# Attention on one Trainium2 core: four logit products issued together with banks of two PSUM pools, and weight transpositions written one block ahead of the value products

## The chip, the core and the metric

The kernel runs on one core of one Trainium2 chip. TensorE (PE) multiplies matrices and writes its results to PSUM, which has eight banks of 512 float32 columns on each of 128 partitions. VectorE (DVE) and ScalarE (ACT) read those banks and compute in SBUF, GpSimd (POOL) adds a little, and DMA queues bring weights from HBM. The metric is the device time of one execution in microseconds; the time of a kernel is the median of its runs.

## What is computed

Two layers of a backbone over 256 context tokens and 256 latent tokens of width 1024. Each layer is a half-step SwiGLU, three token mixers side by side (attention, a gated linear attention and an mLSTM) that are merged by sigmoid gates, and a second half-step SwiGLU. The change touches attention alone. It has 8 query heads of width 64 on 2 key and value heads. Context tokens look at the context; latent tokens look at a window of 128 latent tokens to either side and at the whole context. Each head has a sink logit that takes part in the softmax only. Cut to the latent part:

```python
s_loc = jnp.einsum('bnqhgd,bnkhd->bnhgqk', qb, kb).astype(F32) * scale
s_ctx = jnp.einsum('bnqhgd,bchd->bnhgqc', qb, k_ctx).astype(F32) * scale
s_loc = jnp.where(valid[None, :, None, None], s_loc, -jnp.inf)
p = softmax_with_sink(jnp.concatenate([s_loc, s_ctx], axis=-1), sink_b)
o = (jnp.einsum('bnhgqk,bnkhd->bnqhgd', p_loc, vb)
     + jnp.einsum('bnhgqc,bchd->bnqhgd', p_ctx, v_ctx))
```

## The kernel before

Channels lie on partitions and the 512 tokens (256 of context, then 256 latent) along the free axis. Large products take weights split into a high and a low float32r part and need three matmuls each (`mm3`, lines 258 to 260): high weight by high input, high weight by low input, low weight by high input. A dense product of 128 output channels is 8 x 3 = 24 such matmuls into one bank of the `acc` pool. PSUM's eight banks are shared out in two pools of four: `pacc`, which `acc()` draws from, and `pmx`, which `mx()` draws from and which serves everything small.

The instructions are written in program order; a scheduler then lays out a fixed queue for each engine. It takes the earliest written instruction whose inputs and buffers it expects to be there, so later work that is free goes ahead of earlier work that waits. Between engines semaphores keep the order of data and buffers. On the chip each queue runs in its order.

`attention` (line 1100 on) works in units. A unit is a pair index `a` (0 or 1) and a block of 128 query tokens `qt`: in layer 0, 2 x 4 units, called units 1 to 8 here; in layer 1, where only the latent tokens are wanted, 2 x 2 units, called 1 to 4. Within a group of one `a` the context blocks come first. A unit has four heads: `b` (0, 1) times `kv` (0, 1), where `kv` sets whether rows 0 to 63 or 64 to 127 of the queries `aq[2 * a + b]` and of the keys `kh` are contracted.

- `weights(a, qt)` forms the logits of each head with one matmul (line 1123) of 64 rows into one bank: 256 columns for a context block, 512 for a latent one. It is a float32 product that the trace records as two passes. For a latent block a mask is added (line 1126); then come the maximum (line 1127), its negative against the sink (line 1128), the exponential with its sum on ScalarE (line 1130) into a tile `p` of the 17 tiles of tag `t`, and, after the four heads, the normalisation (lines 1132 to 1138). A logit bank is free once its exponential is done.
- `values(a, qc, nk, pp)` goes over the blocks of 128 keys, two for a context unit and four for a latent one. For each block it transposes the four heads' weights into one bank (line 1147), copies that to SBUF (line 1150 on VectorE for odd blocks, line 1152 on ScalarE for even ones), and multiplies by the values, 64 output channels for each `kv` (line 1154), into the bank `po`, which is copied out at the end (line 1157).
- `fill()` forms one of the eight products of the branch gate "sa" (a dense product into an `acc` bank and a tanh, line 1263); in layer 1 a unit calls for two.

The loop at the end of `attention` writes the weights of a unit, then the fill, then the values of the unit before. The gates, and behind attention the branch "sm", are what the scheduler draws forward where attention waits.

Of the kernel before, what the change touches and what calls it, by code (L numbers as in the profile page):

```python
# [77 lines left out]
def hybrid_backbone_kernel(ctx: ExitStack, tc: tile.TileContext, xT, cc, small, tables, lmask, crow, modw, modt,  # L78
# [20 lines left out]
    def nm(p):  # L99
        cnt[0] += 1  # L100
        return f"{p}{cnt[0]}"
# [4 lines left out]
    def W(dt=F32):  # L106
        return tp.tile([128, T], dt, tag="t", name=nm("t"))

    def O(dt=F32):
        return ox.tile([128, T], dt, tag="x", name=nm("x"))  # L110
# [7 lines left out]
    def mx():  # L118
        return pmx.tile([128, T], F32, tag="mx", name=nm("mx"))

    tt, act, mm = V.tensor_tensor, A.activation, PE.matmul
# [35 lines left out]
    def C(n, i=None, w=128):  # L157
        o, ww = CT[n]
        return ct[:, o:o + ww] if i is None else ct[:, o + i * w:o + (i + 1) * w]
# [13 lines left out]
    def P(l, n, i=0, w=1):  # L173
        o, _ = SM[n]
        return sm[l][:, o + i:o + i + w]
# [896 lines left out]
    def rope(x):  # L1072
        ls = slice(L, T)
        ps = mx()
        mm(ps[:, ls], C("perm"), x[:, ls], True, True)
        t = W()
        tt(t[:, ls], ps[:, ls], C("sin"), ALU.mult)
        tt(x[:, ls], x[:, ls], C("cos"), ALU.mult)
        tt(x[:, ls], x[:, ls], t[:, ls], ALU.add)
# [20 lines left out]
    def attention(l, c0, aq, kh, vt, fill):  # L1100

        rope(kh)
        for i in range(4):
            rope(aq[i])
        nsink = sp.tile([128, 8], F32, tag="nsink", bufs=1, name="nsink%d" % l)
        V.tensor_scalar(nsink[:], P(l, "sink", 0, 8), -1.0, None, ALU.mult)
        sink = P(l, "sink", 0, 8).rearrange("p (v j) -> p v j", v=2)
        ao = [O() for _ in range(4)]

        def weights(a, qt):  # L1110
            lat = qt >= 2
            nk = T if lat else L
            qc = slice(qt * 128, (qt + 1) * 128)
            mx4 = sp.tile([128, 4], F32, tag="mx4", bufs=3, name=nm("mx4"))
            l4 = sp.tile([128, 4], F32, tag="l4", bufs=3, name=nm("l4"))
            e4 = sp.tile([128, 4], F32, tag="e4", bufs=3, name=nm("e4"))
            pp = [None] * 4
            for b in range(2):
                for kv in range(2):
                    h, j = 4 * kv + 2 * a + b, 2 * kv + b  # L1120
                    r = slice(64 * kv, 64 * kv + 64)
                    ps = mx()
                    mm(ps[:, 0:nk], aq[2 * a + b][r, qc], kh[r, 0:nk], True, True)  # L1123
                    if lat:
                        blk = slice(L + 128, T) if qt == 2 else slice(L, L + 128)
                        tt(ps[:, blk], ps[:, blk], C("amask", qt - 2), ALU.add)
                    V.reduce_max(mx4[:, j:j + 1], ps[:, 0:nk], axis=AX.X)
                    V.scalar_tensor_tensor(mx4[:, j:j + 1], mx4[:, j:j + 1], -1.0, nsink[:, h:h + 1], ALU.mult, ALU.min)
                    p = W()
                    act(p[:, 0:nk], ps[:, 0:nk], AF.Exp, bias=mx4[:, j:j + 1], accum_out=l4[:, j:j + 1])  # L1130
                    pp[j] = p
            tt(e4[:].rearrange("p (v j) -> p v j", v=2), sink[:, :, 2 * a:2 * a + 2],
               mx4[:].rearrange("p (v j) -> p v j", v=2), ALU.add)
            act(e4[:], e4[:], AF.Exp)
            tt(l4[:], l4[:], e4[:], ALU.add)
            V.reciprocal(l4[:], l4[:])
            for j in range(4):
                V.tensor_scalar(pp[j][:, 0:nk], pp[j][:, 0:nk], l4[:, j:j + 1], None, ALU.mult)
            return a, qc, nk, pp

        def values(a, qc, nk, pp):
            nb = nk // 128
            po = mx()
            for kb in range(nb):
                pt = mx()
                for j in range(4):
                    PE.transpose(pt[:, j * 128:(j + 1) * 128], pp[j][:, kb * 128:(kb + 1) * 128], C("ident"))  # L1147
                t = W()
                if kb % 2:
                    V.tensor_copy(t[:], pt[:])  # L1150
                else:
                    A.copy(t[:], pt[:])
                for kv in range(2):
                    mm(po[64 * kv:64 * kv + 64, 0:256], vt[:, kb * 128 + 64 * kv:kb * 128 + 64 * kv + 64],  # L1154
                       t[:, 256 * kv:256 * kv + 256], kb == 0, kb == nb - 1)
            for b in range(2):
                V.tensor_copy(ao[2 * a + b][:, qc], po[:, b * 128:(b + 1) * 128])

        last = None
        for a in range(2):  # L1160
            for qt in range(c0 // 128, 4):
                now = weights(a, qt)
                fill()
                if last:
                    values(*last)
                last = now
        fill()
        values(*last)
        return ao

# [349 lines left out]
```

## Time and profile before

| what | value |
|---|---|
| median of 3 runs | 2302.86 us (2300.45 to 2303.84) |
| the profiled execution | 2299.65 us |
| its span, first to last instruction | 2297.5 us |
| TensorE busy | 2269.5 us, 99% of the span |
| VectorE busy | 1532.1 us, 67% |
| ScalarE busy | 970.8 us, 42% |
| attention, layer 0 | about 772 to 859 us |
| attention, layer 1 | about 1988 to 2039 us |

The profile is one execution. A timeline line gives the start of a group of instructions, its length, the engine, the line of the kernel, the operation, output and inputs by the program's names, the shapes (for a matmul rows x columns of the stationary operand first) and how many follow one another without another line between. Matmuls are pipelined: one that starts 0.24 us after the last may be shown as 0.4 us long, so times of TensorE are read from start to start. "PEld" is its loading of weights.

### The profile page before, as it was taken

The page shows a single profiled execution, that of the slowest core. Times are in us where ns is not written, and L with a number is a line of the kernel's source. Part 1 is how long each engine was busy: PE and PEld are TensorE (multiplying, and loading weights), DVE is VectorE, ACT ScalarE, POOL GpSimd, SP SyncE. Part 2 cuts the span into 40 slices and gives each one's busy share as a digit, 9 for nine tenths or more (in the row PEclk, how much of TensorE's full clock was granted, in tenths as well). Part 3 has the DMA queues.
Part 4 walks back from the last instruction along what each step waited for, and adds up shares of the span by engine and source line. Part 5 has one row for each costly group of instructions (what it writes and reads, how often), then busy time and mean ns, then how long its engine had stood idle before and what let it go on. Part 6 is the DMA issues. An engine that isn't in the chain of part 4 may idle for free.

```text
span 2297.5 us, 32871 instructions
## 1 busy us (share of the span) xinstructions
PE 2269.5 (99%) x12494; PEld 1890.6 (82%) x12494; DVE 1532.1 (67%) x3214; ACT 970.8 (42%) x1566; POOL 53.7 (2%) x65
## 2 busy tenths in 40 slices
PE   8999999999999999999999999999999999999999
PEld 4888888877877668888888898888888788889999
DVE  5786875689766763768733357855547897876755
ACT  4322224556545642352222253222246665745443
POOL 0000001000000000200000010000010000001000
PEclk9999999999999999999999999999999999999999
DMA  7655554221212113435532236655433333335764
GB/s 281 220 199 162 193 179 143 92 60 56 83 55 66 63 46 92 156 120 189 172 116 92 83 117 207 200 162 193 152 124 96 90 113 98 125 118 190 233 199 147
DMA packets 140430, 314.94 MB, mean 137 GB/s; under 512 B 30192, under 2 KB 41328, under 8 KB 140144
## 3 DMA queue, kind: packets, MB, share of 16 engines
q1 hardware_dynamic: 139248, 309.69, 41.7%
q0 software_dynamic: 1024, 3.15, 0.4%
q8 instruction: 98, 1.61, 0.3%
q14 instruction: 60, 0.49, 0.1%
HBM read 308.59 MB, written 4.19 MB: 136 GB/s over the span
## 4 chain that ended last, share of the span: by engine, by line
PE 72%; DVE 4%; ACT 2%; DMA 1%; issue 1%; SPq 0%; DVEq 0%; ACTq 0%
PE acc L258 21%; PE acc L259 21%; PE acc L260 20%; PE mx L1123 1%; PE mx L1154 1%; PE mx L1147 1%; DVE lo L225 1%; DMA f<-in_modt_dram 1%; PE mx L1057 1%; PE mx L814 1%; PE mx L988 1%; PE mx L727 1%; PE mx L960 0%; PE mx L1017 0%; PE acc L302 0%
## 5 line engine op out<-in xcount | busy, mean ns | idle before, releaser
L224 ACT CAST hi<-raw 128x1024 fp32r<-128x1024 f32 (+2 forms) x445 | 433.8, 977 | 962.9 <-PE acc L259 623.2
L258 PE MATMUL acc<-xh,hi 128*128 128x512 f32 (+1 forms) x2184 | 779.9, 357 | 5.6 <-ACT xh L629 5.3
L259 PE MATMUL acc<-xl,hi 128*128 128x512 f32 (+1 forms) x2184 | 779.2, 357 | 0.2
L260 PE MATMUL acc<-xh,lo 128*128 128x512 f32 (+1 forms) x2184 | 776.0, 355 | 0.6 <-DVE lo L225 0.6
L225 DVE TENSOR_TENSOR lo<-raw,hi 128x1024 fp32r<-128x1024 f32 (+2 forms) x445 | 502.5, 1132 | 311.1 <-ACT hi L224 302.5
L258 PEld LDWEIGHTS acc<-xh,hi 128*128 128x128 f32 x2184 | 413.5, 189 | 70.8 <-issue 7.0
L259 PEld LDWEIGHTS acc<-xl,hi 128*128 128x128 f32 x2184 | 413.5, 189 | 64.7 <-issue 8.0
L260 PEld LDWEIGHTS acc<-xh,lo 128*128 128x128 f32 x2184 | 413.6, 189 | 62.9 <-issue 5.8
L260 PE MATMUL acc<-f,lo 128*128 128x512 f32 (+1 forms) x896 | 313.7, 350 | 0.0
L258 PE MATMUL acc<-f,hi 128*128 128x512 f32 (+1 forms) x896 | 313.4, 350 | 0.0
L514 DVE SCALAR_TENSOR_TENSOR u<-f,f 128x512 f32<-128x512 f32 x448 | 284.7, 686 | 14.0 <-DMA f<-in_modt_dram 14.0
L259 PE MATMUL acc<-t,hi 128*128 128x512 f32 (+1 forms) x704 | 248.2, 353 | 0.0
L258 PEld LDWEIGHTS acc<-f,hi 128*128 128x128 f32 x896 | 169.4, 189 | 23.2 <-issue 1.2
L260 PEld LDWEIGHTS acc<-f,lo 128*128 128x128 f32 x896 | 169.5, 189 | 22.1 <-issue 0.4
L650 DVE TENSOR_TENSOR t<-t,acc 128x512 f32<-128x512 f32 (+1 forms) x89 | 54.2, 609 | 151.5 <-PE acc L260 150.1
L259 PEld LDWEIGHTS acc<-t,hi 128*128 128x128 f32 x704 | 133.1, 189 | 18.2
L638 DVE SCALAR_TENSOR_TENSOR x<-acc,ggt,x 128x256 f32<-128x256 f32 x136 | 61.2, 480 | 88.1 <-PE acc L260 87.9
L592 POOL TENSOR_TENSOR t<-t,t 128x256 f32<-128x256 f32 x45 | 44.8, 1013 | 1121.4 <-ACT t L588 1121.4
L259 PE MATMUL acc<-x,hi 128*128 128x512 f32 (+1 forms) x192 | 65.3, 342 | 0.0
L314 ACT CAST f<-t 128x512 fp32r<-128x512 f32 (+1 forms) x92 | 51.5, 559 | 20.9 <-DVE t L650 19.2
L629 ACT ACTIVATE xh<-t,mod 128x256 fp32r<-128x256 f32 x88 | 39.3, 500 | 44.2 <-DVE t L628 44.2
L315 DVE TENSOR_TENSOR t<-t,f 128x512 fp32r<-128x512 f32 (+1 forms) x90 | 54.7, 607 | 2.4 <-ACT f L314 2.4
(311 smaller groups left out, 2464.6 us busy)
## 6 DMA issues: line engine op xcount, KB each, us to landing
raw<-in_w_dram SPq DMA_DIRECT2D x179, 512.0 KB, 3.6
f<-in_modt_dram SPq DMA_DIRECT2D x256, 256.0 KB, 4.7
raw<-in_win_dram SPq DMA_DIRECT2D x110, 512.0 KB, 3.5
raw<-in_w_dram SPq DMA_DIRECT2D x61, 384.0 KB, 3.1
raw<-in_w_dram SPq DMA_DIRECT2D x61, 320.0 KB, 2.8
raw<-in_wout_dram SPq DMA_DIRECT2D x16, 512.0 KB, 3.5
raw<-in_wo_dram SPq DMA_DIRECT2D x16, 512.0 KB, 4.0
f<-in_modw_dram SPq DMA_DIRECT2D x16, 256.0 KB, 6.2
```

What stands on the lines that cost most here:

```text
L224: a = A.copy(hi[:, :n], raw[:, :n])
L225: b = V.tensor_tensor(lo[:, :n], raw[:, :n], hi[:, :n].bitcast(F32), ALU.subtract)
L258: mm(o, wh, xh[:, cs], start=first, stop=False)
L259: mm(o, wh, xl[:, cs], start=False, stop=False)
L260: mm(o, wl, xh[:, cs], start=False, stop=last)
L314: A.copy(hi[:, cs], src[:, cs])
L315: tt(lo[:, cs], src[:, cs], hi[:, cs].bitcast(F32), ALU.subtract)
L514: V.scalar_tensor_tensor(junk[:], raw[:], 1.0, cond[s][h][:], ALU.mult, ALU.mult, accum_out=part[:, k, s, h:h + 1])
L592: G.tensor_tensor(sums[c.start][0][:, c], sums[c.start][0][:, c], q[:, c], ALU.add)
L629: a = act(xh[:, c], t[:, c], AF.Identity, bias=sh[:, k, s:s + 1])
L638: V.scalar_tensor_tensor(X[m][:, c], ps[:, c], gate[:, m, s:s + 1], X[m][:, c], ALU.mult, ALU.add)
L650: tt(t[:, c], t[:, c], pb[:, c], ALU.mult)
```

## The change

In `weights` the loop over the four heads is cut in two. The first loop issues the four logit products; the two of `b = 0` take banks of the `mx` pool and the two of `b = 1` banks of the `acc` pool. The second loop does, in the same order of heads, all that came behind a product before. In `values` the product of a block is written behind the next block's transpositions and copy: T0 T1 P0 T2 P1 T3 P2 P3 in place of T0 P0 T1 P1 T2 P2 T3 P3. No instruction is added or left out.

```diff
--- before.py
+++ after.py
@@ -1115,12 +1115,15 @@
             l4 = sp.tile([128, 4], F32, tag="l4", bufs=3, name=nm("l4"))
             e4 = sp.tile([128, 4], F32, tag="e4", bufs=3, name=nm("e4"))
             pp = [None] * 4
+            pss = {}
             for b in range(2):
                 for kv in range(2):
-                    h, j = 4 * kv + 2 * a + b, 2 * kv + b
                     r = slice(64 * kv, 64 * kv + 64)
-                    ps = mx()
+                    ps = pss[b, kv] = (mx, acc)[b]()
                     mm(ps[:, 0:nk], aq[2 * a + b][r, qc], kh[r, 0:nk], True, True)
+            for b in range(2):
+                for kv in range(2):
+                    h, j, ps = 4 * kv + 2 * a + b, 2 * kv + b, pss[b, kv]
                     if lat:
                         blk = slice(L + 128, T) if qt == 2 else slice(L, L + 128)
                         tt(ps[:, blk], ps[:, blk], C("amask", qt - 2), ALU.add)
@@ -1141,6 +1144,13 @@
         def values(a, qc, nk, pp):
             nb = nk // 128
             po = mx()
+
+            def product(kb, t):
+                for kv in range(2):
+                    mm(po[64 * kv:64 * kv + 64, 0:256], vt[:, kb * 128 + 64 * kv:kb * 128 + 64 * kv + 64],
+                       t[:, 256 * kv:256 * kv + 256], kb == 0, kb == nb - 1)
+
+            due = None
             for kb in range(nb):
                 pt = mx()
                 for j in range(4):
@@ -1150,9 +1160,10 @@
                     V.tensor_copy(t[:], pt[:])
                 else:
                     A.copy(t[:], pt[:])
-                for kv in range(2):
-                    mm(po[64 * kv:64 * kv + 64, 0:256], vt[:, kb * 128 + 64 * kv:kb * 128 + 64 * kv + 64],
-                       t[:, 256 * kv:256 * kv + 256], kb == 0, kb == nb - 1)
+                if due:
+                    product(*due)
+                due = kb, t
+            product(*due)
             for b in range(2):
                 V.tensor_copy(ao[2 * a + b][:, qc], po[:, b * 128:(b + 1) * 128])
```

## Rows read from the trace of the kernel before

**Rows 1.** The page, section 1: busy us (share of the span) and instructions of each engine.

```profile
PE 2269.5 (99%) x12494; PEld 1890.6 (82%) x12494; DVE 1532.1 (67%) x3214; ACT 970.8 (42%) x1566; POOL 53.7 (2%) x65
```

**Rows 2.** Windows of the two attention stages: us, busy (instructions) per engine, PEclk, DMA.

```profile
772.00:859.00 87.00, 86.84 (x433) 54.23 (x432) 61.69 (x183) 40.23 (x103) 0.00 (x0) 1.00 0.16 49
1988.00:2039.00 51.00, 50.01 (x337) 36.26 (x336) 43.42 (x115) 25.86 (x60) 0.00 (x0) 1.00 0.25 83
```

**Rows 3.** PE timeline, layer 0, unit 1: start us, us, engine, line, op, out<-in, shapes, count.

```profile
772.54 0.40 PE L258 MATMUL acc<-xh,hi 128*128 128x512 f32 x1
772.86 0.87 PE L1123 MATMUL mx<-f,f 64*128 64x256 f32 x4
...
774.56 0.70 PE L1123 MATMUL mx<-f,f 64*128 64x256 f32 x2
...
775.61 0.70 PE L1123 MATMUL mx<-f,f 64*128 64x256 f32 x2
...
776.57 0.40 PE L258 MATMUL acc<-xh,hi 128*128 128x512 f32 x1
776.81 0.40 PE L259 MATMUL acc<-xl,hi 128*128 128x512 f32 x1
```

**Rows 4.** PE timeline, layer 0, unit 6, four products of 256 columns together.

```profile
820.21 1.42 PE L1123 MATMUL mx<-f,f 64*128 64x256 f32 x8
821.56 0.50 PE L259 MATMUL acc<-xl,hi 128*128 128x512 f32 x1
821.90 0.40 PE L260 MATMUL acc<-xh,lo 128*128 128x512 f32 x1
```

**Rows 5.** PE timeline, layer 0, unit 8, four products of 512 columns, one and three.

```profile
839.97 1.12 PE L1123 MATMUL mx<-f,f 64*128 64x512 f32 x2
841.03 0.65 PE L1154 MATMUL mx<-t,f 128*64 128x256 f32 x4
841.61 2.18 PE L1123 MATMUL mx<-f,f 64*128 64x512 f32 x6
843.72 0.50 PE L259 MATMUL acc<-xl,hi 128*128 128x512 f32 x1
```

**Rows 6.** PE timeline, layer 1, unit 2's first and last neighbours, and unit 4's run.

```profile
1993.53 0.28 PE L260 MATMUL acc<-xh,lo 128*128 128x256 f32 x1
...
1999.36 0.28 PE L259 MATMUL acc<-xl,hi 128*128 128x256 f32 x1
...
2020.57 2.53 PE L1123 MATMUL mx<-f,f 64*128 64x512 f32 x8
2023.04 0.39 PE L258 MATMUL acc<-f,hi 128*128 128x256 f32 x1
```

**Rows 7.** PE timeline, layer 1: the two stalls, idle us and releaser in brackets.

```profile
2016.85 0.65 PE L1154 MATMUL mx<-t,f 128*64 128x256 f32 x4 [0.49 <-ACT t L1152]
...
2023.93 0.66 PE L1147 MATMUL mx<-ct,t 128*128 128x128 f32 x4 [0.51 <-ACT t L1130]
```

**Rows 8.** PE timeline, layer 0: a dense product, then values of four blocks.

```profile
849.54 0.40 PE L258 MATMUL acc<-xh,hi 128*128 128x512 f32 x1
849.87 0.65 PE L1154 MATMUL mx<-t,f 128*64 128x256 f32 x4
850.46 1.53 PE L1147 MATMUL mx<-ct,t 128*128 128x128 f32 x12
851.91 1.52 PE L1154 MATMUL mx<-t,f 128*64 128x256 f32 x12
```

**Rows 9.** DVE, then ACT timeline, layer 0, unit 4: one head's softmax.

```profile
800.63 0.29 DVE L1126 TENSOR_TENSOR mx<-mx,ct 128x128 f32<-128x128 f32 x1
...
800.95 0.69 DVE L1127 TENSOR_REDUCE mx<-mx 128x1 f32<-128x512 f32 x1
801.68 0.16 DVE L1128 SCALAR_TENSOR_TENSOR mx<-mx,nsink 128x1 f32<-128x1 f32 x1
...
801.87 0.69 ACT L1130 ACTIVATE t<-mx,mx 128x512 f32<-128x512 f32 x1
```

## The prediction

> **What bounds the kernel now.** Read the page's busy times first: TensorE is busy for 2269.5 of the 2297.5 us span [rows 1], so work on other engines pays only where TensorE waits for it. Then cut out the two stretches in which attention runs. In both windows TensorE is busy nearly throughout: 86.84 of 87 us in layer 0 and 50.01 of 51 us in layer 1, with the clock at 1.00 (2.4 GHz), while VectorE has 25 and 8 us free [rows 2]. Nothing in 138 us waits long for logits or transposes, since products of the branch gates (lines 258 to 260) fill the gaps. So the change can shorten only two things: the 1.1 us of waits, nearly all of it two stalls of 0.49 and 0.51 us in layer 1 [rows 7], and the time that TensorE spends on the attention's own matmuls.
>
> The second is not fixed, which the TensorE timeline shows. A logit product contracts over 64 rows, kv 0 on rows 0 to 63 and kv 1 on rows 64 to 127, and is recorded as two passes. In layer 0, unit 8, one product alone takes 1.06 us to the next start (839.97 to 841.03) and three take 2.11 us [rows 5]. In layer 1, unit 4, four take 2.47 us [rows 6], far below four times 1.06: neighbours on different halves overlap. A product split off from its partner loses that, and also pays at both ends. Between two gate matmuls the starts lie 0.24 us apart [rows 3]. From one to the start of a weight-times-value product it is 0.33 us [rows 8], so 0.09 more. After a logit run the first two gate matmuls lie 0.34 us apart [rows 4], so 0.10 more.
>
> **The change part by part.** No instruction is added or removed: 48 logit products, 160 transpositions, 80 value products and their copies stay, and so do all DMAs and the SP queue. What changes is the order asked for, and the banks.
>
> Logits. Before, all four banks of a unit come from the mx pool, where the banks of the previous unit's logits and of its values come free one at a time. That shows as three patterns. Layer 0, unit 1 runs 2, 1, 1 products of 256 columns: 4.03 us from the gate matmul ahead (772.54) to the one behind (776.57), with six gate starts in it, counting the first [rows 3]. Less 6 x 0.24 that leaves 2.59 us. Unit 6 has its four together: 821.90 less 820.21 less one gate interval is 1.45 us [rows 4], plus 0.09 in front, 1.54. Gain 1.05 us; unit 2 (1, 2, 1) I take alike. Five units of 512 columns have one or two products apart from the rest (units 3, 4, 7 and 8 of layer 0, unit 3 of layer 1). Unit 8 stands for them: 1.06 + 2.11 = 3.17 us [rows 5] against 2.47 [rows 6], gain 0.70 each, 3.50 in all. Layer 1, unit 2 runs 1, 2, 1 among gates: 5.83 us from 1993.53 to 1999.36 with 14 gate starts [rows 6], these at 0.12 us (256 columns, half of 0.24), leaves 4.15 us; four together are 2.47 + 0.09 + 0.10 = 2.66, gain 1.49. The other four units already have a run of four: gain 0. Sum: 2 x 1.05 + 3.50 + 1.49 = 7.1 us.
>
> From this I take back what two pools can break. The mx pair and the acc pair need not come free at the same moment; where they come apart there is one boundary more, 0.09 + 0.11 = 0.20 us (the 0.11 is worked out below). I allow it in six units, 1.2 us, and one unit that stays split, 0.7 us. No row shows a logit in an acc bank; the bounds are 0 (all runs whole) and the whole 7.1 us (every gain lost).
>
> A rule on this overlap: by the Trainium skill (TensorE: Matmul & The Clock Gate, Measured speedup vs the span model), tiles on different rows cost about 4 ns each beyond the first. By it a run of four is two times 1.06 us, 2.12, where the trace has 2.47 [rows 6]; the six units of 512 columns that gain would give 2.1 us more, and the time would be 2295.9. I keep the row.
>
> Values. Before, the trace already does not follow the written order: in a unit of four blocks it runs one block's transpositions, its products, then three blocks' transpositions (1.45 us from 850.46 to 851.91) and three blocks' products [rows 8]: two runs of value products. In a run a block's transpositions cost 1.45 / 3 = 0.48 us; the single block's products take 0.59 (849.87 to 850.46), so leaving a run costs 0.11 and entering it 0.09: 0.20 per run. The new order asks for T0 T1 P0 T2 P1 T3 P2 P3; with some of it drawn together as before I expect three runs of products, one more, in the eight units of four blocks: +1.6 us. In the four units of two blocks T0 P0 T1 P1 becomes T0 T1 P0 P1, a run fewer: -0.8 us. Net +0.8. Bounds: -0.8 (only the short units change) to +4 (two more runs in each long unit, 3.2, and 0.8 for the short ones).
>
> By the Trainium skill (TensorEngine Tiling (Array Packing), Key Properties), changing the tiling mode drains TensorE, and a value product (64 columns) is another mode than a transposition. This speaks against an order that alternates more; it agrees with the 0.20 us above and gives no price of its own.
>
> Stalls. A block's copy out of its bank lies between its transpositions and its products; the 0.49 us stall is on such a copy [rows 7]. A block of lead covers that one; the 0.51 us stall is on an exponential, which no part of the change moves up. I take -0.5 us (bounds 0 and -1.0). One more t buffer is live per unit, of 17; I cost it at nothing.
>
> The added wait. Gate products take acc banks, and two of the four now belong to a unit's logits until their exponentials are done. A gate's first matmul that finds no bank holds up all that stands behind it on TensorE's queue: transpositions, value products, later logits, and through these the ScalarE and VectorE copies. One head costs VectorE 0.29 + 0.69 + 0.16 = 1.14 us and ScalarE 0.69 [rows 9], so the last of four is done about 4 x 1.14 + 0.69 = 5.3 us after the run. A gate product of 24 matmuls takes 24 x 0.24 = 5.8 us on one bank, and a bank is left for the next. Cost 0 while one unit's logits hold acc banks.
>
> **Sum.** -7.1 + 1.2 + 0.7 + 0.8 - 0.5 = -4.9 us. On the profiled execution's own 2299.65 us that is 2294.75; it lies 3.2 us under the median of the runs, so on the median 2302.86 I forecast 2298.0, -0.21%. Everything behind attention shifts forward with it, as TensorE is busy there too [rows 1].
>
> **The rivals.**
> Banks still come one by one. The mx pool served the values between two units' logits; the acc pool has only gates there, so a later unit's logits can take each acc bank as an exponential frees it, 1.14 us apart [rows 9], and go out alone. The patterns 2, 1, 1 and 1, 3 [rows 3, 5] show that products do go out singly when banks do. Against it: TensorE has higher-placed work in that time. Then the 7.1 us are not gained and up to two of the units that ran whole split (1.05 + 1.49 at most): 2302.86 + 0.8 - 0.5, with 0 to 2.5 more, 2303 to 2306; middle 2304.
>
> Gates are starved, and it is slower. If the next unit's acc logits go out early too, all four acc banks are logits and no gate product can start, for the 5.3 us to the last exponential. A long unit's values give TensorE about 4 x (0.48 + 0.48) = 3.9 us meanwhile, so 1.4 us idle in each of eight, about 0.6 in each of four short ones: 13.6 us. Less 4.9 that is +8.7: 2311.6. It decides from the point where two units' logits hold acc banks at once. For it: logits depend on nothing but banks. Against it: a gate is asked for between any two units. The Trainium skill names that pressure (TensorEngine Tiling (Array Packing), Gotcha 1: PSUM Pressure): row tiles need different banks.
>
> The values alternate as written, with late copies. Two more runs in the eight long units (3.2 in place of 1.6) and a stall as in [rows 7], 0.5, in each of twelve units: -4.9 + 1.6 + 6.0 = +2.7, 2305.6.
>
> All parts hold: runs whole everywhere, -0.8 for the values, both stalls gone: -7.1 - 0.8 - 1.0 = -8.9, 2294.0.
>
> **How the numbers follow.** Chances: forecast 0.46 (2295.5 to 2300.5), banks one by one 0.25, all parts hold 0.11, alternating values 0.08, starved gates 0.10. 0.2% is 4.6 us, about what a measurement of this kernel can tell from no change: faster is below 2298.3, slower above 2307.5. The time by the Trainium skill's rule on overlap, 2295.9, gets 0.02 of the forecast's 0.46, as the trace has a run of four at 2.47 us [rows 6]. The forecast lies at the edge of faster; I give two thirds of its case to faster. Faster: 0.31 + 0.11 = 0.42. Slower: 0.10 and a little of the second case and fourth, 0.12. Same: 0.46. The range goes from 2293.0 (all parts hold, less the 1 us that runs differ by) to 2306.5 (the upper end of the one-by-one and alternating cases); starved gates lie outside. The likeliest case alone is 2295.5 to 2300.5.
>
> **What would show it.** Runs of eight passes of line 1123, or two of four, in all twelve units, and a first window shorter by about 4 us, say the logits part is right; single products of two passes among gates say the banks rival. Value products (line 1154) in three runs or fewer per long unit confirm the +0.8. TensorE idle before a gate's first matmul, released by the exponential of line 1130, is the starved case. The forecast is wrong if the stretches behind attention do not move up, or if new stalls in attention exceed 2 us.

## The result and the profile after

The changed kernel takes 2316.95 us in the median of its runs (2315.23 to 2320.63), against 2302.15 us for the kernel before in runs on the same chip: a ratio of 1.0072, 95% interval 1.006 to 1.0085. It is slower by about 15 us. I had forecast 2298.0 us with a range up to 2306.5, so the time lies outside the range and on the other side of no change.

The profiled execution took 2315.23 us, with a span of 2313.3 us against 2297.5 before, 15.8 us more. The page's first line, and then windows (length in us, busy us and instructions of TensorE, its weight loads, VectorE, ScalarE and GpSimd, then the granted clock, the DMA share and GB/s), first the two of [rows 2], then a part of the stretch ahead of layer 1's attention:

```profile
PE 2273.7 (98%) x12494; PEld 1891.4 (82%) x12494; DVE 1530.7 (66%) x3214; ACT 970.8 (42%) x1566; POOL 53.6 (2%) x65
...
772.00:859.00 87.00, 81.66 (x409) 52.68 (x407) 57.16 (x175) 38.90 (x102) 0.00 (x0) 0.98 0.15 49
1988.00:2039.00 51.00, 50.49 (x337) 36.93 (x337) 39.79 (x102) 27.69 (x62) 0.00 (x0) 0.95 0.27 83
...
1968.00:1976.00 8.00, 4.69 (x32) 3.86 (x31) 6.93 (x12) 7.88 (x14) 0.00 (x0) 0.98 0.44 139
1976.00:1988.00 12.00, 7.70 (x16) 4.36 (x18) 8.66 (x24) 6.67 (x14) 0.00 (x0) 0.50 0.10 39
```

The last two of these windows before the change:

```profile
1968.00:1976.00 8.00, 8.00 (x63) 7.63 (x62) 5.82 (x11) 7.94 (x14) 0.00 (x0) 1.00 0.56 164
1976.00:1988.00 12.00, 12.00 (x90) 11.51 (x89) 9.63 (x18) 9.98 (x20) 0.00 (x0) 1.00 0.49 154
```

The instruction counts on TensorE are equal (12494), and its busy time rose by only 4.2 us. Layer 0's window lost 5.2 us of TensorE's time (86.84 to 81.66). In the window of layer 1's attention, where I had looked, TensorE lost no busy time, though part of that window runs at a lower clock (0.95 on average). The large loss lies ahead of it: from 1976 to 1988 TensorE issued 16 matmuls where it had issued 90, and its clock was granted at 0.50 (1.2 GHz).

To place the 15.8 us I take three landmarks that both kernels pass, the first matmul of line 1067 (the norm of the keys of layer 0), the last of line 727 (just ahead of layer 1's attention stretch) and the last of line 622 (behind layer 1's mixer). The views of these lines on TensorE, after (line, operation, count, shortest, median and longest ns, first and last start in us):

```profile
L1067 PE MATMUL mx<-t,ct x20: 379/592/796, 736.9 to 1980.7; 128*128 128x512 f32 x12, 128*128 128x256 f32 x8
L727 PE MATMUL mx<-t,ones_h x32: 379/538/697, 500.5 to 1961.1; 128*128 128x512 f32 x16, 128*128 128x256 f32 x16
L622 PE MATMUL mx<-t,ones_d x54: 377/378/483, 387.7 to 2112.6; 128*128 128x256 f32 x54
```

and before:

```profile
L1067 PE MATMUL mx<-t,ct x20: 379/592/697, 737.7 to 1978.3; 128*128 128x512 f32 x12, 128*128 128x256 f32 x8
L727 PE MATMUL mx<-t,ones_h x32: 379/538/697, 501.2 to 1956.9; 128*128 128x512 f32 x16, 128*128 128x256 f32 x16
L622 PE MATMUL mx<-t,ones_d x54: 377/378/484, 388.4 to 2095.8; 128*128 128x256 f32 x54
```

The first landmark comes 0.8 us earlier, the second 4.2 us later, the third 16.8 us later. So stretch A (first to second, with layer 0's attention) is 5.0 us longer, stretch B (second to third, with layer 1's attention) 12.6 us, and the rest 1.8 us shorter. Every kernel below is read by the same two stretches, each from one profiled execution.

**Layer 1.** The waits of TensorE from 1890 to 2045 us (line waited at, releaser: us in total, times, longest), where before had only the two stalls of [rows 7]:

```profile
PE mx L1067 <- ACT t L1065: 6.3, 3, 2.6
PE mx L1075 <- DVE t L1077: 0.9, 1, 0.9
PE mx L1075 <- DVE f L1069: 0.5, 1, 0.5
PE mx L1150 <- ACT t L1162: 0.2, 1, 0.2
PE mx L1150 <- DVE t L1160: 0.2, 1, 0.2
```

Lines 1065 to 1079 are the norm of the queries and their rotary embedding, the preparation of attention. These are chains of short steps between TensorE, ScalarE and VectorE, and they were there before as well. What stood between them on TensorE is gone. The TensorE timeline of after:

```profile
1971.71 0.28 PE L260 MATMUL acc<-xh,lo 128*128 128x256 f32 x1
1973.54 0.70 PE L1067 MATMUL mx<-t,ct 128*128 128x256 f32 x2 [1.55 <-ACT t L1065]
1976.85 1.22 PE L1067 MATMUL mx<-t,ct 128*128 128x256 f32 x2 [2.61 <-ACT t L1065]
1980.16 1.22 PE L1067 MATMUL mx<-t,ct 128*128 128x256 f32 x2 [2.09 <-ACT t L1065]
...
1987.67 2.08 PE L1123 MATMUL mx<-f,f 64*128 64x512 f32 x4
1989.54 1.91 PE L1123 MATMUL acc<-f,f 64*128 64x512 f32 x4
1991.38 0.58 PE L258 MATMUL acc<-xh,hi 128*128 128x256 f32 x1
```

From 1971.71, the end of the last query projection, to 1991.38 no dense product runs at all. Before, gate products filled that time. No gate waits for a bank in that stretch; the gates stand behind it in TensorE's fixed order, so it was the scheduler that held them back. The acc banks were not occupied: VectorE copies the last projection out of its bank at 1972.03. But the first unit's two acc logits are written ahead of any gate product, and they are ready only when the rotary embedding is done, at 1987.67. My reading is that the pool's banks are given in the order in which the program asks for them, so that a gate product asked for behind these two logits waits for them although it needs nothing from them.

The clock fell too, within the second of these three waits. The window 1975.70:1992.80 shows 0.50 throughout with 12.5 us busy. Unit 1's run of four products takes 3.71 us there (1987.67 to 1991.38), where unit 2's, at full clock, takes 1.92. By that ratio the 12.5 us of work would take about half, so up to 6.2 us went to the clock. Unit 2's run:

```profile
1997.94 1.13 PE L1123 MATMUL mx<-f,f 64*128 64x512 f32 x4
1998.90 1.02 PE L1123 MATMUL acc<-f,f 64*128 64x512 f32 x4
1999.86 0.39 PE L258 MATMUL acc<-xh,hi 128*128 128x256 f32 x1
```

In the window 1940:2070 idle time of TensorE rose from 1.00 to 8.11 us. 7.1 us of idle time and up to 6.2 us of clock make 13.3; stretch B grew by 12.6. So the matmuls themselves gained 0.7 us at most.

**Layer 0.** The TensorE timeline:

```profile
770.10 0.70 PE L1123 MATMUL acc<-f,f 64*128 64x256 f32 x2
...
771.35 0.70 PE L1123 MATMUL mx<-f,f 64*128 64x256 f32 x4
772.98 0.70 PE L1123 MATMUL acc<-f,f 64*128 64x256 f32 x2 [0.93 <-ACT f L1274]
773.34 1.36 PE L1123 MATMUL mx<-f,f 64*128 64x256 f32 x4
777.26 0.50 PE L258 MATMUL acc<-xh,hi 128*128 128x512 f32 x1 [2.56 <-ACT t L1133]
```

Another acc pair had gone out at 760.90. With the products at 770.10 and 772.98 that makes four, all four acc banks, for units 1 and 2. The second unit's last one waits for a gate's tanh (line 1274) to free a bank, and then the gate product at 777.26 waits 2.56 us for an exponential (line 1133). From 777.7 to 781.1 the clock is at 0.50 again. Four more waits of value products on VectorE's copies (line 1160) make 1.8 us. In the window 745:885 idle time rose from 0.17 to 5.34 us, and 3.4 us at half clock lose 1.7. Stretch A grew by 5.0, so the matmuls gained 5.2 + 1.7 - 5.0 = 1.9 us, if nothing else in it changed.

From unit 3 on gates stand between any two units, and no unit starves them. Logits go out in pairs, apart from each other, but not always: the mx pairs of units 5 and 6 and the acc pairs of layer 1's units 3 and 4 are split. Value products alternate with transpositions. Unit 3's values, with the logits of unit 5 among them (a product of two passes is one alone):

```profile
805.26 1.03 PE L1157 MATMUL mx<-ct,t 128*128 128x128 f32 x8
806.22 0.70 PE L1123 MATMUL acc<-f,f 64*128 64x256 f32 x4
806.85 0.50 PE L258 MATMUL acc<-xh,hi 128*128 128x512 f32 x1
807.30 0.65 PE L1150 MATMUL mx<-t,f 128*64 128x256 f32 x4
807.88 0.65 PE L1157 MATMUL mx<-ct,t 128*128 128x128 f32 x4
808.58 0.65 PE L1150 MATMUL mx<-t,f 128*64 128x256 f32 x4
809.16 0.66 PE L1157 MATMUL mx<-ct,t 128*128 128x128 f32 x4
809.75 0.65 PE L1150 MATMUL mx<-t,f 128*64 128x256 f32 x4
810.33 0.70 PE L1123 MATMUL mx<-f,f 64*128 64x256 f32 x2
810.96 0.65 PE L1150 MATMUL mx<-t,f 128*64 128x256 f32 x4
811.54 0.70 PE L1123 MATMUL mx<-f,f 64*128 64x256 f32 x2
```

### The profile page after: what moved, and what is told of

The parts are those of the page before. It is cut to its first block, busy times and chain, and to the rows that moved or that the text cites. A ratio compares the mean times of both kernels' runs of the same rounds, so it can differ in the third digit from the quotient of the medians.

```text
span 2313.3 us, 32870 instructions
## 1 busy us (share of the span) xinstructions
PE 2273.7 (98%) x12494; PEld 1891.4 (82%) x12494; DVE 1530.7 (66%) x3214; ACT 970.8 (42%) x1566; POOL 53.6 (2%) x65
## 4 chain that ended last, share of the span: by engine, by line
PE 71%; DVE 5%; ACT 3%; issue 1%; DVEq 0%; ACTq 0%
PE acc L258 21%; PE acc L259 20%; PE acc L260 20%; DVE lo L225 1%; PE mx L1150 1%; ACT hi L224 1%; PE mx L1057 1%; PE mx L1157 1%; PE mx L814 1%; PE mx L988 1%; PE mx L727 1%; PE mx L960 0%; PE mx L1123 0%; PE mx L1017 0%; PE acc L302 0%
```

## The experiments

The theory after the result: logits in acc banks starve the gate products, ahead of attention because they are asked for first, and at its start because two units' logits fill the pool. The rivals: the value order costs as much, or the split loop does; or the starving is a matter of written order alone, and asking for gates first mends it. Times in us; "before" is the median of the kernel before on the same chip. A and B are the changes of the two stretches against the profile before, each from one execution; idle is what TensorE leaves of the windows 745:885 and 1940:2070 (before: 0.17 and 1.00).

| kernel | median | before | ratio (95%) | A | B | idle |
|---|---|---|---|---|---|---|
| after | 2316.95 | 2302.15 | 1.0072 (1.006 to 1.0085) | +5.0 | +12.6 | 5.34, 8.11 |
| values alone | 2304.34 | 2301.13 | 1.0014 (1.0004 to 1.0023) | +2.4 | +1.4 | 1.16, 0.07 |
| banks alone | 2314.73 | 2301.13 | 1.0061 (1.0044 to 1.0078) | +2.5 | +11.9 | 5.74, 8.66 |
| after, gates ahead | 2311.66 | 2301.13 | 1.0049 (1.0034 to 1.0064) | +1.0 | +11.7 | 3.25, 4.62 |
| banks alone, gates ahead | 2308.21 | 2301.13 | 1.0031 (1.0017 to 1.0046) | -2.3 | +8.5 | 3.98, 7.90 |
| the same, in layer 0 only | 2298.69 | 2300.80 | 0.9993 (0.9984 to 1.0002) | -0.9 | 0.0 | 4.00, 0.99 |
| banks alone, fewer gates ahead | 2305.63 | 2300.80 | 1.0021 (1.0012 to 1.003) | -2.9 | +8.5 | 2.61, 5.89 |
| before, gates ahead | 2298.61 | 2300.80 | 0.9989 (0.998 to 0.9998) | -2.9 | 0.0 | 0.14, 2.38 |
| one acc bank, gates ahead | 2301.91 | 2300.80 | 1.0006 (0.9997 to 1.0015) | -1.2 | +2.6 | 0.32, 2.25 |
| before, other gates ahead | 2299.30 | 2300.91 | 0.9994 (0.9985 to 1.0003) | -1.7 | +0.4 | 0.34, 0.26 |

**Values alone.** All four banks from the mx pool again, the rest as in after.

```diff
-                    ps = pss[b, kv] = (mx, acc)[b]()
+                    ps = pss[b, kv] = mx()
```

> All four logit banks come from the mx pool again; the values stay a block ahead. Theory A (gate products queue in the acc pool behind logits written before them, and TensorE starves before and at the start of attention): the starving goes, TensorE idle in attention falls from 13.4 us (5.3 and 8.1) to under 4, time 2300 to 2307. Theory B (the alternating values with late copies cost the time): 2312 to 2318.

Measured 2304.34, 3.2 us above before. No wait of the starved kind is left, and B grew by 1.4 us only. So the values, with the split logit loop that this kernel keeps, cost about 3 us: four times the 0.8 of my sum, and inside its bounds. The trace shows one wait of 1.1 us on a copy and more changes between kinds of matmul; the loop was not measured apart from them.

**Banks alone.** After's logits, before's values.

```diff
...
-                if due:
-                    product(*due)
-                due = kb, t
-            product(*due)
+                for kv in range(2):
+                    mm(po[64 * kv:64 * kv + 64, 0:256], vt[:, kb * 128 + 64 * kv:kb * 128 + 64 * kv + 64],
+                       t[:, 256 * kv:256 * kv + 256], kb == 0, kb == nb - 1)
```

> Two banks of a unit come from the acc pool as in the changed kernel; the values are written as before. Theory A: the idle before attention in layer 1 (about 7 us and half clock for 17 us) and at its start in layer 0 (3.5 us) stay, time 2311 to 2317. Theory B: the cost goes with the values, 2296 to 2302.

Measured 2314.73: 13.6 us above before, of the 14.8 that the whole change cost. Its long waits are those of after, 6.3 us at line 1067 among them. The parts add up in the profiles: A 2.4 + 2.5 = 4.9 against 5.0, B 1.4 + 11.9 = 13.3 against 12.6; by the medians they make 16.8 against 14.8. So the banks carry the loss. This kernel also shows what the logits part is worth: in layer 0 idle rose by 5.6 us and half clock lost 1.7, yet the stretch grew by 2.5, so its matmuls gained 5.6 + 1.7 - 2.5 = 4.8 us, if nothing else in the stretch changed.

**After, gates ahead.** Two of the eight gate products of layer 0 and six of layer 1 are asked for ahead of the units.

```diff
+        for _ in range(2 if c0 == 0 else 3):
+            fill()
         last = None
```

> The changed kernel with two gate products in layer 0 and six in layer 1 written ahead of the first unit, so that their acc banks are asked for before any logit's. Theory A: the idle in front of attention is gone in both layers, window of layer 1 back near the kernel before, time 2298 to 2306. Theory B: as the changed kernel, 2312 to 2318.

Measured 2311.66, 5.7 us above the upper end that I gave. The wait ahead of attention is gone, as expected: no wait at line 1067 is left in the waits of 1955 to 2045 us. But the loss in stretch B is nearly whole (11.7 of 12.6), as TensorE now waits inside attention. Its waits there:

```profile
PE acc L258 <- ACT t L1133: 2.8, 1, 2.8
...
PE acc L1123 <- ACT t L1133: 0.4, 1, 0.4
```

and the windows at half clock:

```profile
2003.70:2014.00 10.30, 9.87 (x27) 4.11 (x28) 6.87 (x24) 4.13 (x11) 0.00 (x0) 0.50 0.03 12
2020.80:2024.20 3.40, 3.18 (x15) 2.72 (x15) 2.02 (x6) 1.40 (x6) 0.00 (x0) 0.50 0.00 0
```

13.05 us of work at half clock lose 6.5 us, more than the 3.6 us by which idle time rose. Written order alone is not the whole cause, then; the theory of order as I had put it fell here.

**Banks alone, gates ahead.** The same two lines added to the kernel with the banks alone.

> As the gates-ahead kernel, but the values written as before: acc banks and gates ahead alone. Theory A: no starving, logits in pairs, no more value runs than before: 2294 to 2302. Theory B: below the kernel before, 2294 to 2301, and equal to the banks-alone kernel.

Measured 2308.21, 6.2 us above the expected range, with runs spread from 2304.25 to 2313.80; the profiled one took 2304.55. Stretch A is 2.3 us shorter than before. In B the waits stand in the middle of attention:

```profile
2003.85 2.74 PE L1123 MATMUL acc<-f,f 64*128 64x512 f32 x4 [2.18 <-ACT t L1133]
...
2016.59 0.39 PE L258 MATMUL acc<-xh,hi 128*128 128x256 f32 x1 [2.74 <-ACT t L1133]
...
2027.68 0.38 PE L258 MATMUL acc<-xh,hi 128*128 128x256 f32 x1 [1.40 <-ACT t L1133]
```

All three wait for an exponential to free an acc bank: twice a dense product waits for a unit's logits, once logits wait for those of the unit before. The eight gates run out early here: six ahead and two behind unit 1 leave none to be asked for between units 2, 3 and 4, so logits of two units meet. In layer 0 two ahead and one for each of units 1 to 6 leave none behind unit 7, and the next dense product waits 1.92 us for an exponential (841.78). This is the rival of the prediction at its decision point, two units' logits in the four banks.

**The same, in layer 0 only.** Layer 1 as before.

```diff
-                    ps = pss[b, kv] = (mx, acc)[b]()
+                    ps = pss[b, kv] = (mx, acc if c0 == 0 else mx)[b]()
...
-        for _ in range(2 if c0 == 0 else 3):
+        for _ in range(2 if c0 == 0 else 0):
```

> The gates-ahead banks-alone kernel in layer 0 (two gates ahead, acc banks, old values); layer 1 as in the kernel before. Theory A (all of the cost comes from acc logits standing before gates): layer 0 keeps its 2.3 us gain, layer 1 costs nothing: 2297 to 2301. Rival (the pairs gain nothing, the run was a low one): 2301 to 2304.

Measured 2298.69, not to be told from before. B is 0.0: without acc banks in layer 1 its whole loss is gone. TensorE's order in layer 0 is that of the last kernel, but A is -0.9 here and -2.3 there. A stretch at half clock makes the difference, here first, then the last kernel:

```profile
843.00:846.00 3.00, 3.00 (x11) 1.52 (x12) 1.86 (x5) 0.00 (x0) 0.00 (x0) 0.50 0.02 5
```

```profile
843.00:846.00 3.00, 3.00 (x18) 1.11 (x16) 2.60 (x6) 0.00 (x0) 0.00 (x0) 1.00 0.02 5
```

TensorE is busy throughout in both. Both come shortly behind the same wait of 1.92 us for an exponential, which ends at 841.41 here and at 841.78 in the last kernel. Why the clock fell behind it in one execution and not in the other stays open.

**Banks alone, fewer gates ahead.** One gate product in layer 0 and two in layer 1.

```diff
+        for _ in range(1 if c0 == 0 else 1):
+            fill()
```

> Banks alone with the old values, and one gate ahead in layer 0, two in layer 1 (none in the banks-alone kernel, two and six in the gates-ahead one). Theory A: each gate written ahead takes its 2.9 us out of the starving before attention in layer 1, so layer 1 costs 5 to 8 us in place of 12, layer 0 about -1 to +1: 2305 to 2310. If the starving is not a matter of what is written first: 2313 to 2316.

Measured 2305.63, inside the expected range, though partly by luck: layer 1 cost 8.5 us where I expected 5 to 8, and layer 0 gained 2.9 where I expected 1 at most. The wait ahead of layer 1's attention goes with the number of gates asked for first: 6.3 us with none, 3.1 with two, 0 with six. Gate products now stand behind the first two norms (1968.00 and 1972.27), and the third stands alone:

```profile
1968.00 0.70 PE L1067 MATMUL mx<-t,ct 128*128 128x256 f32 x2
...
1976.52 1.22 PE L1067 MATMUL mx<-t,ct 128*128 128x256 f32 x2 [3.09 <-ACT t L1065]
```

Just the gates written ahead of the first logits run there, and none that are written behind them, which is what banks given in written order would do. B is +8.5 here as with six gates ahead, where the wait in front is gone: what six gates save in front is lost inside.

**Before, gates ahead.** No other change: six gate products of layer 1 and two of layer 0 asked for first.

> The kernel before with two gates ahead in layer 0 and six in layer 1, nothing else: all logits from the mx pool, old values. Theory A: no starving by logits, since none is in acc; fewer single logit products at the start: 2297 to 2302. If gates written ahead themselves starve the later units: layer 1 5 us or more longer, 2305 to 2310.

Measured 2298.61, 2.2 us below before (0.9989, interval 0.998 to 0.9998): the lowest median of the study, level with the 2298.69 above, and below both kernels of the case. Stretch A alone gains. Units 1 and 2 of layer 0, which were split (unit 1 in [rows 3]), now go out whole, from mx banks. Unit 2:

```profile
784.53 1.13 PE L1123 MATMUL mx<-f,f 64*128 64x256 f32 x8
785.59 0.50 PE L258 MATMUL acc<-xh,hi 128*128 128x512 f32 x1
```

So part of what the change was for is to be had without the acc pool. B is 0.0, so the lead of the gates by itself is not what costs layer 1 its time in the kernels above.

**One acc bank, gates ahead.** Only a unit's last logit product takes an acc bank; values as before, gates ahead as in the kernel with the banks alone.

```diff
-                    ps = pss[b, kv] = (mx, acc)[b]()
+                    ps = pss[b, kv] = (acc if b and kv else mx)()
```

> As the gates-ahead banks-alone kernel, but only one logit of a unit from the acc pool. Theory A1 (occupancy: four acc banks full of logits until their exponentials are done): two units hold two banks, gates always find one, waits of line 258 for the exponential (6 us in two layers) go: 2297 to 2303. Theory A2 (only the order in which banks are asked for counts): the waits stay, 2304 to 2309.

Measured 2301.91 against 2308.21 with two. No dense product waits for an exponential any more, in either layer, and B falls from +8.5 to +2.6. How many acc banks the logits hold is therefore a cause of its own beside the order. What is left of B goes with a wait of 1.79 us for a unit's weights and a clock of 0.50 from 2001 to 2007 behind it.

**Before, other gates ahead.** Three gates ahead in layer 0, four in layer 1.

```diff
+        for _ in range(3 if c0 == 0 else 2):
+            fill()
```

> The kernel before with three gates ahead in layer 0 and four in layer 1, nothing else. Theory A: as the gates-ahead-alone kernel, with layer 0's first two units whole (-2 to -3 us) and without that kernel's 1.8 us wait for an exponential in layer 1: 2296 to 2300. If a lead of gates does nothing by itself: 2300 to 2302.

Measured 2299.30, interval 0.9985 to 1.0003: inside the expected range, but no gain over the other numbers of gates, and not to be told from before. That kernel's wait of 1.8 us in layer 1 is gone, and B is no better for it.

## Why the prediction was wrong

**The step that failed** is "the added wait", which ends in "Cost 0 while one unit's logits hold acc banks". In after it was worth 3.5 us of waits in layer 0 (0.93 and 2.56) and 7.7 in layer 1 (6.3, 0.9 and 0.5), with 1.7 and up to 6.2 us of clock: up to 19 us in place of 0. Shorter matmuls hid a part, so that the banks alone cost 13.6 us net. Two things were missing from the step.

First, I looked at who holds a bank and not at who has asked for one. The step reckons from the moment a unit's logits run (5.3 us to the last exponential). But the first unit's acc logits were in the pool's line of requests before they could run, and in layer 1 that was 16 us long, from the last projection at 1971.71 to 1987.67. I had cut the windows of [rows 2] from the first logits on, so the preparation of attention, which gates were covering, was outside of everything I priced. The banks alone (waits of 6.3, then 3.1 and 0 with two and six gates ahead) and layer 0 alone (B 0.0) show that the acc logits of layer 1 cause it. That requests are served in written order is inferred from which gates ran where; no row shows a bank's owner.

Second, I priced idle time and not the clock behind it. In layer 1 the idle time rose by 7.1 us, and 12.5 us of work at 0.50 cost up to 6.2 us more. The sign that I had set for starving, TensorE idle before a gate's first matmul until an exponential, appears in layer 0 (2.56 us); in layer 1 the waits stand at line 1067 and are released by line 1065, which I had not thought of.

**The rivals.** "Gates are starved, and it is slower" had the kind right and named the point that decides, two units' logits in the acc pool, which the four banks at 772.98 and the 2.56 us wait behind them show. I gave it 0.10. Its place and price were off: it expected 1.4 us in each long unit and 0.6 in each short one, 2311.6 us. In after, the middle units are not starved at all, just as the argument against it said ("a gate is asked for between any two units"); the loss stands at the start of layer 0 and ahead of layer 1. The mid-attention form it described appeared only with gates ahead. "Banks still come one by one" came in part: in after four units from unit 3 of layer 0 on have a split pair, among them the acc pairs of layer 1's units 3 and 4; it was acc banks that the rival named. "The values alternate as written" was right in its pattern in layer 0, four runs of products in the long unit shown; its stall of 0.5 us in each of twelve units was not: the waits on copies make 2.2 us in all.

**Logits.** This step held in size in layer 0, as far as one profile tells. Layer 0's share was 2 x 1.05 + 4 x 0.70 = 4.9 us, and the banks alone measured 4.8. Part of this is chance, as two sizes were off in opposite ways. A run that is whole is shorter than I took it: four products of 512 columns take 1.92 us at full clock, not 2.47 [rows 6], and four of 256 take 1.06 to the next start, not 1.35 [rows 4]. Against that, nearly every unit of layer 0 has its two pairs apart, where I allowed for six in all. On the rule of the Trainium skill (TensorE: Matmul & The Clock Gate, Measured speedup vs the span model), which made a run of four 2.12 us: I kept the row of 2.47, and the measured 1.92 us lies below both.

**Values.** I took one run of value products more in each long unit; the unit shown of after has two more (four against the two of [rows 8]). So have six of the eight long units, while units 1 and 2 of layer 1 have none more; the four short ones have one fewer each, as I took it. That is eight runs more, an estimate of 1.6 us at the 0.20 us of the prediction, and waits on copies come on top. Measured with the split loop it is 3.2 us, against +0.8 in the sum. The bounds, up to 4, held. The error is 2.4 us, a sixth of the whole.

**Stalls.** The two of [rows 7] are gone in after, as taken (-0.5, bound -1.0), and new ones took their place: 1.8 us on copies in layer 0, 0.4 in layer 1.

**What stays open.** What a wait costs in clock is not settled. Behind a wait of 1.92 us the clock fell in the kernel with acc banks in layer 0 only and not in the one before it, and in that one, in layer 1, the wait of 2.74 us at 2016.59 left it at 1.00. The spread of that kernel, banks alone with gates ahead, over 9.5 us goes with the clock: its runs of 2304.25 and 2304.55 us have a mean granted clock of 0.998, the one of 2313.80 has 0.992. Why a run of four takes 2.47 us in some units and 1.92 in others was not tested. In the trace's single starts the run at 1997.94 has its eight passes in four pairs 0.01 us apart, the one of [rows 6] only its first two pairs.

## What to carry to other kernels

Before a tile with a long wait is moved to a pool that serves filler work, ask from when it will be in line for a bank, not only how long it holds one: filler asked for behind it may stop until its inputs exist. Look for what the filler covers outside the stretch that is being tuned, and price idle time of a busy TensorE with the clock that it may lose. Asking for some filler ahead of the first such tile was worth a little by itself here, with the banks left alone (2.2 us with one lead; 1.6 us, not to be told from nothing, with another).

## What the runs showed of the hardware that was not expected

In a kernel that is 98% busy the clock fell to 0.50 (1.2 GHz) within the second of two idle stretches, of 1.55 and 2.61 us, and stayed there for 17.1 us, with three shorter ones (2.09, 0.85 and 0.50) among them. The run of four products took 3.71 us there against 1.92 at full clock. A single wait of 2.56 us in layer 0 was followed by 3.4 us at 0.50, while the 2.74 us of the kernel with banks alone and gates ahead left the clock at 1.00. In the kernel after with gates ahead the 13.05 us of work at half clock cost 6.5 us, more than the idle time that had been added (3.6 us).
